# Shift and scale of adaLN with the weight tiles as the stationary operand, and a bank and a load size changed elsewhere, in a decoder-trunk kernel

## The chip, the cores and the metric

The kernel runs on one core of one Trainium2 chip. The metric is the device time of one execution in microseconds (us). It was measured three times for the kernel before.

## What is computed

One layer of a hybrid decoder trunk, for a prompt of 1024 tokens and 8 samples of 8 tokens (1088 columns in all). The part that the change touches most is the front of the layer:

```python
mod = jax.nn.silu(c) @ w_ada + b_ada
shift, scale, gate = jnp.split(mod, 3, axis=-1)
h = _rmsnorm(x, norm_g) * (1.0 + scale[:, None, :]) + shift[:, None, :]
parts = jnp.split(h @ w_in, _in_offsets(), axis=-1)
```

`c` has nine rows (one prompt, eight samples) of 1024; `w_ada` is 1024 x 3072. After that come three groups of dilated window attention, a state-space (SSD) branch whose output has a group RMSNorm over four groups, the two branch projections, the merge, and `x + gate * (merged @ w_out)` with a last RMSNorm.

## The kernel before

Everything is float32. The large products (`w_in`, `w_ssm`, `w_att`, `w_out`) are made of three products of a high and a low part in the type fp32r; `load_w` (lines 185 to 193) loads a weight tile and splits it on ACT and DVE. Small products run in plain float32, and the trace then shows two records (a weight load, PEld, and a matmul, PE) for one matmul of the code.

**Stage 0** (pool `ph0`, lines 291 to 368) makes `h`. Eight tiles `xT` (128 features x 1088 tokens) are squared on ACT, summed over features by PE (`sums`, line 165), and a root is taken (`rms`, `rsqrt`); PE spreads it over partitions into `rb` (line 356). `ada(q)` for q = 0 to 3 makes shift and scale of 256 features each. It loads two tiles `wa` of 1 MB and runs 32 matmuls (line 316): the stationary operand is `scT`, SiLU of the conditioning, 32 columns wide (nine of them filled), the moving operand is 128 columns of `w_ada`, and the four blocks j sit beside each other in four column groups of the array. So the result has sequences on partitions; ACT copies it (`row`, line 318), PE transposes it (line 320), and DVE adds and multiplies the biases into `mod` (lines 327 to 329). `modulate(f)` then makes `h_hi[f]` and `h_lo[f]` of one feature tile on DVE, ACT and POOL. `project_early` (line 242) begins two of the 96 projections of `w_in` while `h` is still being made: 144 matmuls that go through the feature tiles in pairs, 36 matmuls for two tiles.

Here and in the output stage the order of instructions is chosen by a scheduler ahead of time; each engine then works through its own list in order. All loads and stores are issued on one queue (SP), which holds eight transfers at a time.

**Attention and SSD** (a region in which PE's order is the order of the code, and in which the class `Order` mixes the small matmuls of the side branch into the stream of the projections by modelled costs). PSUM has eight banks; in the SSD part three belong to the projections (`bankPJ`), two to `bankA`, three to `bankB`, each handed round in turn. At the end of each of the four SSD groups PE sums squares (`sums`, line 165, called at line 967) into a bank named `ms`; DVE reads it at line 170. The next matmuls of the side branch are the transposes `tt` of the next group (three banks of `bankB`), later `cb` (two banks of `bankA`, one of `bankB`).

**Output stage** (lines 1114 on): five passes over eight column tiles. In pass 1, `ada_gate` (lines 466 to 480) makes the gate from eight tiles `wg` of 512 KB that share one buffer with the tile `smp`, which is filled in pass 4.

Of the kernel before, what the change touches and what calls it, by code (L numbers as in the profile page):

```python
# [9 lines left out]
F32 = mybir.dt.float32  # L10
F32R = mybir.dt.float32r
AF = mybir.ActivationFunctionType
# [4 lines left out]
D = 1024  # L17
T = 1024
# [92 lines left out]
def trunk(ctx: ExitStack, tc: tile.TileContext, I, O):  # L111
# [180 lines left out]
    with pool("ph0", 2) as p0:  # L292
# [13 lines left out]

        def ada(q):

            pr = bankB("ada")
            for k in range(0, 8, 4):  # L310
                wa = p0.tile([128, 4, 4, 128], F32, tag="wa", name="wa", bufs=6)
                SP.dma_start(out=wa.rearrange("p k j n -> p k (j n)"),
                             in_=I["w_ada"][q, k:k + 4].rearrange("k p n -> p k n"))
                for i in range(4):
                    for j in range(4):
                        PE.matmul(pr[j * 32:j * 32 + 32, :128], scT[:, k + i, :], wa[:, i, j, :], start=k + i == 0, stop=k + i == 7)
            row = p0.tile([128, 128], F32, tag="row", name="row")
            S.activation(row, pr[:, :128], AF.Copy)
            pt = bankB("adaT")
            PE.transpose(pt[:, :128], row, ident)  # L320
            fs = slice(2 * q, 2 * q + 2)
            pt = pt[:, :128].rearrange("p (i c n) -> p i c n", i=2, c=2)

            def each(ap):
                return ap[:, fs, None].to_broadcast([128, 2, 9])

            V.tensor_tensor(mod[:, 1, fs, :], pt[:, 1, :, :9], each(bs), op=OP.add)
            V.tensor_tensor(mod[:, 1, fs, :], mod[:, 1, fs, :], each(P("norm_g")), op=OP.mult)
            V.tensor_tensor(mod[:, 0, fs, :], pt[:, 0, :, :9], each(P("b_ada")), op=OP.add)
# [135 lines left out]

    def ada_gate(pool_, wgp, k, pg):

        wg = wgp.tile([128, D], F32, tag="smp", name="wg")
        SP.dma_start(out=wg, in_=I["w_gate"][k])
        for j in range(4):  # L470
            PE.matmul(pg[j * 32:j * 32 + 32, :256], scT[:, k, :], wg[:, j * 256:(j + 1) * 256], start=k == 0, stop=k == 7)
        if k < 7:
            return
        gt = pool_.tile([128, 256], F32, tag="gt", name="gt", bufs=1)
# [364 lines left out]
    with ExitStack() as bctx:  # L839
# [100 lines left out]
        def side():  # L940
            for gr in range(4):
# [21 lines left out]
                    order.passed.add(("x", xt))  # L963

                yield 7000.0,
                ps = bankB("ms")
                sums(ps, sq)
                ms = bp.tile([128, 3, QT], F32, tag="ms", name="ms", bufs=1)
                rms(ms, ps, 512)
# [151 lines left out]
    with pool("yr", 2) as yr, pool("yw", 2) as yw:  # L1121
# [27 lines left out]
        wlo = acp.tile([128, KO, D], F32R, name="wolo")  # L1149
        cut_psum("out", p=4, a=4)  # L1150
        pg = bankA("gate")
        mhi, mlo = [], []
        for gr in range(5):
            if gr:
                if gr < 4:
# [7 lines left out]
            for m in range(8):  # L1163
# [25 lines left out]
                if gr == 4:  # L1189

                    a, b = split(acc[m], 0.5)
                    mhi.append(a)
                    mlo.append(b)

                    if m == 0:
                        smp = acp.tile([128, KO, 2 * TS], F32R, tag="smp", name="smp")
                    S.activation(smp[:, m, :TS], a[:, T:].bitcast(F32), AF.Copy)
                    S.activation(smp[:, m, TS:], b[:, T:].bitcast(F32), AF.Copy)


    fp = ctx.enter_context(pool("fin", 1))
# [7 lines left out]
    for t in range(9):  # L1209
# [8 lines left out]
        for i in range(m):  # L1218
            ps = bankA("fo")
            cs = slice(i * w, (i + 1) * w)  # L1220
            if t == 8:

                for k in range(KO):
                    PE.matmul(ps[:, :w], smp[:, k, :], whi[:, k, cs], start=k == 0, stop=k == KO - 1)
                low = f2.tile([TS, w], F32, tag="low", name="low")
                S.activation(low, ps[TS:, :w], AF.Copy)
                V.tensor_tensor(low, low, gbs[:, cs], op=OP.mult)
                V.tensor_tensor(x[:n, cs], x[:n, cs], low, op=OP.add)
                for k in range(KO):
                    PE.matmul(ps[:n, :w], smp[:, k, :TS], wlo[:, k, cs], start=False, stop=k == KO - 1,  # L1230
                              skip_group_check=True)
            ps = ps[:n, :w]
            for k in range(KO if t < 8 else 0):
# [168 lines left out]
```

## Time and profile before

| what | value |
|---|---|
| median of 3 runs | 1892.5 us |
| lowest and highest | 1889.75, 1894.63 us |
| the profiled execution, its own time | 1892.67 us |
| its span, first to last instruction | 1890.6 us |
| time outside the span | 2.07 us |
| PE busy | 1853.4 us, 98% |
| DVE, ACT, POOL busy | 1020.6, 663.4, 271.5 us |
| mean granted TensorE clock | 0.994 of 2.4 GHz |

The profile is of one execution. A page gives busy times by engine and the costliest groups; the trace behind it is asked for stretches of time (windows), for waits, for a tile's instructions, and for the instructions in order of time (timeline). PE is TensorE's matmuls, PEld its weight loads, SPq the queue that issues transfers. A group of matmuls in a timeline row has its start, its length and its count (x32).

### The profile page before, as it was taken

How to read it: one execution, taken by the hardware profiler on the slowest of the kernel's cores; microseconds unless marked ns; L12 is line 12 of the kernel's file. 1: busy time of each engine (PE TensorE's matmuls, PEld its weight loads, DVE VectorE, ACT ScalarE, POOL GpSimd, SP SyncE). 2: the span in 40 equal slices, each digit the busy share in tenths (PEclk: the TensorE clock that was granted, in tenths of full speed). 3: DMA queues.
4: the chain of work that ended last, by engine and by line, in shares of the span. 5: the costliest groups of instructions: out<-in, count | busy, mean ns of one | idle time of the engine just before them, and what ended most of it. 6: DMA issues, size and time to landing. Idle time of an engine off the chain costs nothing.

```text
span 1890.6 us, 32497 instructions
## 1 busy us (share of the span) xinstructions
PE 1853.4 (98%) x13217; PEld 1736.5 (92%) x13217; DVE 1020.6 (54%) x1983; ACT 663.4 (35%) x1275; POOL 271.5 (14%) x445
## 2 busy tenths in 40 slices
PE   6999999999999999999999999999999999999998
PEld 4999999998999999999999999999999989999986
DVE  4633343325324322566776677577758656566655
ACT  4444223323423342423452435243534332131222
POOL 3100000000000000122322231233224200000400
PEclk8999999999999999999999999999999999999999
DMA  8422462273256227435453544443333364364322
GB/s 335 141 80 94 151 213 69 89 227 132 98 160 199 84 91 245 144 92 190 149 160 108 183 152 138 128 151 119 106 104 108 122 225 156 123 197 150 121 89 78
DMA packets 108870, 269.55 MB, mean 143 GB/s; under 512 B 41501, under 2 KB 50513, under 8 KB 105457
## 3 DMA queue, kind: packets, MB, share of 16 engines
q1 hardware_dynamic: 108720, 267.48, 43.1%
q8 instruction: 104, 1.70, 0.4%
q14 instruction: 46, 0.37, 0.1%
HBM read 224.93 MB, written 80.26 MB: 161 GB/s over the span
## 4 chain that ended last, share of the span: by engine, by line
PE 90%; DMA 5%; DVE 2%; issue 1%; ACT 1%; SPq 0%; POOL 0%; ACTq 0%; DVEq 0%
PE pj L198 23%; PE pj L199 22%; PE pj L200 22%; PE s L207 2%; PE o L207 2%; DMA csb<-cs_d 2%; PE pt L211 2%; PE yd L207 2%; PE yo L207 2%; PE fo L1237 2%; PE fo L1238 2%; PE fo L1236 2%; PE stt L207 1%; PE early L242 1%; PE tt L211 1%
## 5 line engine op out<-in xcount | busy, mean ns | idle before, releaser
L198 PE MATMUL pj<-h_hi,whi 128*128 128x368 f32 x2256 | 755.9, 335 | 0.4 <-ACT raw L870 0.4
L200 PE MATMUL pj<-h_lo,whi 128*128 128x368 f32 x2256 | 739.1, 328 | 0.0
L199 PE MATMUL pj<-h_hi,wlo 128*128 128x368 f32 x2256 | 738.9, 328 | 0.0
L198 PEld LDWEIGHTS pj<-h_hi,whi 128*128 128x128 f32 x2256 | 425.0, 188 | 17.1 <-issue 13.6
L199 PEld LDWEIGHTS pj<-h_hi,wlo 128*128 128x128 f32 x2256 | 424.9, 188 | 0.0
L200 PEld LDWEIGHTS pj<-h_lo,whi 128*128 128x128 f32 x2256 | 424.4, 188 | 0.0
L192 DVE TENSOR_TENSOR wlo<-wraw,whi 128x1024 fp32r<-128x1024 f32 (+1 forms) x136 | 149.8, 1101 | 191.0 <-ACT whi L191 189.0
L191 ACT ACTIVATE whi<-wraw 128x1024 fp32r<-128x1024 f32 (+1 forms) x136 | 126.5, 930 | 336.8 <-PE pj L200 283.6
L198 PE MATMUL pj<-yhi,whi 128*128 128x368 f32 (+1 forms) x480 | 157.3, 328 | 1.4 <-ACT yhi L1125 1.2
L199 PE MATMUL pj<-yhi,wlo 128*128 128x368 f32 (+1 forms) x480 | 157.6, 328 | 0.2 <-DVE wlo L192 0.2
L200 PE MATMUL pj<-ylo,whi 128*128 128x368 f32 (+1 forms) x480 | 155.6, 327 | 0.0
L649 DVE COPY pT<-pt 128x512 f32<-128x512 f32 x40 | 27.6, 690 | 147.4 <-PE pt L211 74.9
L630 ACT ACTIVATE pr<-pr,st 128x128 f32<-128x128 f32 (+1 forms) x192 | 83.6, 438 | 46.8 <-DVE st L627 46.8
L198 PEld LDWEIGHTS pj<-yhi,whi 128*128 128x128 f32 x480 | 90.1, 188 | 3.3 <-ACT yhi L1125 2.0
L199 PEld LDWEIGHTS pj<-yhi,wlo 128*128 128x128 f32 x480 | 90.1, 188 | 3.0 <-issue 2.1
L200 PEld LDWEIGHTS pj<-ylo,whi 128*128 128x128 f32 x480 | 89.9, 188 | 0.0
L887 DVE SCALAR_TENSOR_TENSOR xc<-raw,cw,xc 128x1112 f32<-128x1112 f32 x60 | 83.0, 1383 | 11.8 <-ACT xc L885 10.8
L980 DVE TENSOR_TENSOR csb<-tok,csb 128x2048 f32<-128x2048 f32 x16 | 37.1, 2317 | 75.1 <-DMA csb<-cs_d 75.1
L506 DVE COPY k<-pj 128x368 f32<-128x368 f32 (+2 forms) x44 | 23.9, 579 | 73.9 <-PE pj L200 70.7
L1011 POOL TENSOR_TENSOR xde<-xdt,tok 128x256 f32<-128x256 f32 x64 | 43.6, 709 | 133.8 <-DVE xdt L1004 133.8
L1067 POOL TENSOR_TENSOR sst<-sst,eall 128x256 f32<-128x256 f32 x64 | 49.9, 810 | 69.9 <-PE yo L207 67.6
L1034 DVE SCALAR_TENSOR_TENSOR sta<-sta,eall,stt 128x64 f32<-128x64 f32 x224 | 45.1, 271 | 26.8 <-ACT sta L1030 26.8
(275 smaller groups left out, 2396.4 us busy)
## 6 DMA issues: line engine op xcount, KB each, us to landing
wraw<-in_w_in SPq DMA_DIRECT2D x96, 512.0 KB
csb<-cs_d SPq DMA_DIRECT2D x16, 1088.0 KB
kt<-in_kc SPq DMA_DIRECT2D x32, 448.0 KB
out_kc<-in_kc SPq DMA_DIRECT2D x32, 448.0 KB
out_vc<-in_vc SPq DMA_DIRECT2D x28, 512.0 KB
vt<-in_vc SPq DMA_DIRECT2D x28, 512.0 KB
sg_d<-sg SPq DMA_DIRECT2D x16, 544.0 KB
ecs<-cs_d SPq DMA_DIRECT2D x32, 272.0 KB
```

The source lines that it names most:

```text
L191: S.activation(hi, raw, AF.Copy)
L192: V.tensor_sub(lo, raw, hi.bitcast(F32))
L198: PE.matmul(ps, whi[:, k, :], xhi[k], start=first and k == 0, stop=False)
L199: PE.matmul(ps, wlo[:, k, :], xhi[k], start=False, stop=False)
L200: PE.matmul(ps, whi[:, k, :], xlo[k], start=False, stop=last and k == n - 1)
L207: PE.matmul(out, w, x, **kw)
L211: PE.transpose(out, x, eye)
L630: S.activation(pr[:, h, c0:c0 + m], pr[:, h, c0:c0 + m], AF.Exp, scale=-1.0, bias=st[:, 0, h, u:u + 1], accum_out=st[:, 1, h, u:u + 1])
L887: V.scalar_tensor_tensor(c, raw[:, t:t + CONV], cw[:, j, t:t + 1], c, op0=OP.mult, op1=OP.add)
L1011: G.tensor_tensor(xde[:, c:c + 2].rearrange("p c (h d) -> p c h d", h=2), xdt[:, c:c + 2, :].rearrange("p c (h d) -> p c h d", h=2), tok[: ...
L1034: V.scalar_tensor_tensor(sta[:, i, hs], sta[:, i - 1, hs], eall[:, h0 + h, i:i + 1], ps[:, c, hs], op0=OP.mult, op1=OP.add)
L1067: G.tensor_tensor(part, part, etot[:, h0:h0 + 2, b:b + 2].rearrange("n h b -> n b h")[:, :, :, None] .to_broadcast([128, 2, 2, 64]), op=OP ...
```

## The change

In `ada` the weight tile `wa[:, i, j, :]` becomes the stationary operand, 128 columns, and the nine filled columns of `scT` move. The result has features on partitions, so the copy `row` and the transpose are gone, and one bank of `bankB` is used for each q in place of two. The sums at the end of an SSD group go to `bankA`. The gate's tiles are loaded in halves of 256 KB into two buffers, and `smp` is cut into two tiles accordingly.

```diff
         def ada(q):
-            pr = bankB("ada")
+            pt = bankB("ada")
             for k in range(0, 8, 4):
                 wa = p0.tile([128, 4, 4, 128], F32, tag="wa", name="wa", bufs=6)
...
                 for i in range(4):
                     for j in range(4):
-                        PE.matmul(pr[j * 32:j * 32 + 32, :128], scT[:, k + i, :], wa[:, i, j, :], start=k + i == 0, stop=k + i == 7)
-            row = p0.tile([128, 128], F32, tag="row", name="row")
-            S.activation(row, pr[:, :128], AF.Copy)
-            pt = bankB("adaT")
-            PE.transpose(pt[:, :128], row, ident)
+                        PE.matmul(pt[:, j * 32:j * 32 + 9], wa[:, i, j, :], scT[:, k + i, :9], start=k + i + j == 0,
+                                  stop=k + i == 7, skip_group_check=True)
...
-        wg = wgp.tile([128, D], F32, tag="smp", name="wg")
-        SP.dma_start(out=wg, in_=I["w_gate"][k])
-        for j in range(4):
-            PE.matmul(pg[j * 32:j * 32 + 32, :256], scT[:, k, :], wg[:, j * 256:(j + 1) * 256], start=k == 0, stop=k == 7)
+        for i in range(2):
+            wg = wgp.tile([128, D // 2], F32, tag="smp", name="wg", bufs=2)
+            SP.dma_start(out=wg, in_=I["w_gate"][k][:, i * 512:(i + 1) * 512])
+            for j in range(2 * i, 2 * i + 2):
+                PE.matmul(pg[j * 32:j * 32 + 32, :256], scT[:, k, :], wg[:, j % 2 * 256:(j % 2 + 1) * 256], start=k == 0,
+                          stop=k == 7)
...
                 yield 7000.0,
-                ps = bankB("ms")
+                ps = bankA("ms")
                 sums(ps, sq)
...
-                    if m == 0:
-                        smp = acp.tile([128, KO, 2 * TS], F32R, tag="smp", name="smp")
-                    S.activation(smp[:, m, :TS], a[:, T:].bitcast(F32), AF.Copy)
-                    S.activation(smp[:, m, TS:], b[:, T:].bitcast(F32), AF.Copy)
+                    if m % 4 == 0:
+                        smp.append(acp.tile([128, 4, 2 * TS], F32R, tag="smp", name="smp", bufs=2))
+                    S.activation(smp[-1][:, m % 4, :TS], a[:, T:].bitcast(F32), AF.Copy)
+                    S.activation(smp[-1][:, m % 4, TS:], b[:, T:].bitcast(F32), AF.Copy)
```

The change also moves instructions. PE's list in stage 0 before, from the sums of `x` on (`ms`): the first two `ada` blocks, then the first projections. The other two `ada` blocks follow after 19 and after 44 of the 144 matmuls of `early`.

```order
L165 MATMUL ms<-sqk,onesc 32x272 x32
L316 MATMUL ada<-wa,scT 32x128 x32
L356 MATMUL rb<-ms,onesc 128x272 x4
L320 MATMUL adaT<-pack,row 128x128
L316 MATMUL ada<-wa,scT 32x128 x32
L242 MATMUL early_459<-h_hi_90,whi 128x368
```

The same place in the changed kernel (its line 317 is the matmul of `ada`, 354 that of `rb`):

```order
L165 MATMUL ms<-sqk,onesc 32x272 x32
L317 MATMUL ada<-scT,wa 128x9 x20
L354 MATMUL rb<-ms,onesc 128x272
L317 MATMUL ada<-scT,wa 128x9 x2
L354 MATMUL rb<-ms,onesc 128x272
L317 MATMUL ada<-scT,wa 128x9 x2
L354 MATMUL rb<-ms,onesc 128x272
L317 MATMUL ada<-scT,wa 128x9 x2
L354 MATMUL rb<-ms,onesc 128x272
L317 MATMUL ada<-scT,wa 128x9 x102
L242 MATMUL early_443<-h_hi_90,whi 128x368
```

All 128 matmuls of `ada` now stand ahead of the first matmul of `early`.

PE's list between two SSD groups before, with the engines whose semaphores a row waits for in brackets (`ms` are the sums, `tt` the next group's transposes):

```order
L200 MATMUL pj<-h_lo_100,whi 128x368
L165 MATMUL ms<-sq,onesc 32x272 [waits Pool_49] x4
L211 MATMUL tt<-pack,xc 128x128 [waits DVE_49]
L211 MATMUL tt<-pack,xc 128x128 x7
L211 MATMUL tt<-pack,xcs 128x128 [waits DVE_49]
L198 MATMUL pj<-h_hi_93,whi 128x368
```

And now:

```order
L200 MATMUL pj<-h_lo_100,whi 128x368
L165 MATMUL ms<-sq,onesc 32x272 [waits DVE_49,Pool_49]
L165 MATMUL ms<-sq,onesc 32x272 [waits Pool_49] x3
L211 MATMUL tt<-pack,xc 128x128 [waits DVE_49]
L211 MATMUL tt<-pack,xc 128x128 x7
L211 MATMUL tt<-pack,xcs 128x128
```

The order is the same; the last transpose waits for nobody, and the first sum now waits for DVE too.

SP's list where the gate's loads begin, in the output stage, before (`yx` and `rb` feed the operands of the next pass, `wraw` is a weight tile):

```order
L469 DMA wg<-in_w_gate 128x1024
L1139 DMA yx<-u_d 128x1088
L1134 DMA rb<-rs_d 128x1088
L469 DMA wg<-in_w_gate 128x1024
L1139 DMA yx<-u_d 128x1088
L469 DMA wg<-in_w_gate 128x1024
```

And now:

```order
L468 DMA wg<-in_w_gate 128x512 x2
L1139 DMA yx<-u_d 128x1088
L468 DMA wg<-in_w_gate 128x512
L1134 DMA rb<-rs_d 128x1088
L468 DMA wg<-in_w_gate 128x512
L1139 DMA yx<-u_d 128x1088
L468 DMA wg<-in_w_gate 128x512
```

Two halves are asked for at the place of the first whole tile; the third and the fourth stand on both sides of `rb`.

## Rows read from the trace of the kernel before

**Rows 1.** The page, part 1: busy us, share, instructions.

```profile
PE 1853.4 (98%) x13217; PEld 1736.5 (92%) x13217; DVE 1020.6 (54%) x1983; ACT 663.4 (35%) x1275; POOL 271.5 (14%) x445
```

**Rows 2.** The chain of waits, 0 to 70 us: start, length, what.

```profile
13.20 16.52 DMA wa<-in_w_ada
56.35 6.23 PE early L242 x36
```

**Rows 3.** Timeline of PE, 17 to 37 us: start, length, operation, [idle before, releaser].

```profile
18.06 1.93 PE L316 MATMUL ada<-wa,scT 128*32 128x128 f32 x32 [1.17 <-DMA wa<-in_w_ada]
...
29.76 1.94 PE L316 MATMUL ada<-wa,scT 128*32 128x128 f32 x32 [0.70 <-DMA wa<-in_w_ada]
```

**Rows 4.** Timeline, 51 to 58 us: the last pair of feature tiles.

```profile
51.48 0.17 DVE L327 TENSOR_TENSOR mod<-adaT,bs 128x18 f32<-128x18 f32 x1
...
55.16 2.18 ACT L339 ACTIVATE h_hi<-xT,mod 128x1024 fp32r<-128x1024 f32 x2
```

**Rows 5.** Tile ada in 17.9:20.2, 20.6:22.6, 27:29.3, 36.8:38.8: ns min/median/max, starts.

```profile
L316 PEld LDWEIGHTS ada<-wa,scT x32: 127/177/178, 18.0 to 19.4; 128*32 128x32 f32 x32
...
L316 PEld LDWEIGHTS ada<-wa,scT x32: 110/168/177, 20.7 to 21.9; 128*32 128x32 f32 x32
...
L316 PEld LDWEIGHTS ada<-wa,scT x32: 125/177/177, 27.1 to 28.4; 128*32 128x32 f32 x32
...
L316 PEld LDWEIGHTS ada<-wa,scT x64: 106/110/110, 36.9 to 38.4; 128*32 128x32 f32 x64
```

**Rows 6.** Tile early in 31:36 and in 40:62.5: weight loads, ns.

```profile
L242 PEld LDWEIGHTS early<-h_hi,whi x8: 288/329/338, 31.6 to 34.9; 128*128 128x128 f32 x8
...
L242 PEld LDWEIGHTS early<-h_hi,whi x36: 186/188/189, 41.8 to 59.1; 128*128 128x128 f32 x36
```

**Rows 7.** Windows: length, busy us PE, PEld, DVE, ACT, POOL; clock, DMA, GB/s.

```profile
27.10:29.00 1.90, 1.87 (x32) 1.51 (x32) 1.77 (x5) 0.00 (x0) 1.53 (x3) 0.50 1.04 384
...
31.60:35.60 4.00, 4.00 (x17) 3.98 (x14) 1.35 (x2) 0.69 (x4) 3.71 (x10) 0.51 1.04 394
35.60:41.80 6.20, 6.19 (x90) 5.47 (x88) 3.05 (x5) 1.57 (x4) 3.63 (x6) 1.00 1.04 392
```

**Rows 8.** Timeline of the weight loads, 802.5 to 805 us.

```profile
802.62 1.92 PEld L207 LDWEIGHTS cb<-CT,xc 128*128 128x128 f32 x16
...
804.46 0.30 PEld L207 LDWEIGHTS cb<-CTs,xcs 128*128 128x128 f32 x2
...
804.68 0.19 PEld L198 LDWEIGHTS pj<-h_hi,whi 128*128 128x128 f32 x1
```

**Rows 9.** Windows, the end of the first transfers.

```profile
42.00:43.00 1.00, 1.00 (x7) 1.00 (x8) 1.00 (x1) 0.99 (x1) 0.00 (x0) 1.00 0.44 172
```

**Rows 10.** Waits of PE, 765 to 1530 us: total, times, longest.

```profile
PE tt L211 <- DVE ms L170: 5.9, 3, 2.6
```

**Rows 11.** Timeline, 968 to 990 us: the change from one SSD group to the next.

```profile
972.29 0.43 DVE L170 TENSOR_SCALAR ms<-ms 128x272 f32<-128x272 f32 x1
...
972.77 0.33 PE L211 MATMUL tt<-pack,xcs 128*128 128x128 f32 x1 [1.84 <-DVE ms L170]
...
987.35 1.95 PE L207 MATMUL cb<-CT,xc 128*128 128x128 f32 x16
```

**Rows 12.** Windows around two of those waits.

```profile
970.75:974.16 3.41, 1.57 (x11) 1.39 (x10) 1.97 (x4) 2.90 (x3) 0.54 (x2) 1.00 0.52 105
974.16:977.58 3.42, 3.42 (x13) 3.42 (x12) 2.75 (x2) 3.39 (x5) 0.00 (x0) 0.50 0.69 277
...
1158.48:1161.90 3.42, 3.42 (x13) 3.42 (x13) 1.89 (x2) 3.40 (x5) 0.00 (x0) 0.50 0.88 307
```

**Rows 13.** Waits of PE, 1500 to 1891 us; timeline at the first gate load.

```profile
PE gate L471 <- DMA wg<-in_w_gate: 3.1, 2, 1.7
...
1539.02 0.33 SPq L469 DMA_DIRECT2D wg<-in_w_gate  x1
...
1543.65 0.64 PE L471 MATMUL gate<-wg,scT 128*32 128x256 f32 x8 [1.65 <-DMA wg<-in_w_gate]
```

More of the change, by code (lines that the diff above doesn't have):

```diff
@@ L1151, in trunk @@
         pg = bankA("gate")
-        mhi, mlo = [], []
+        mhi, mlo, smp = [], [], []
         for gr in range(5):
@@ L1223, in trunk @@
                 for k in range(KO):
-                    PE.matmul(ps[:, :w], smp[:, k, :], whi[:, k, cs], start=k == 0, stop=k == KO - 1)
+                    PE.matmul(ps[:, :w], smp[k // 4][:, k % 4, :], whi[:, k, cs], start=k == 0, stop=k == KO - 1)
                 low = f2.tile([TS, w], F32, tag="low", name="low")
@@ L1229, in trunk @@
                 for k in range(KO):
-                    PE.matmul(ps[:n, :w], smp[:, k, :TS], wlo[:, k, cs], start=False, stop=k == KO - 1,
+                    PE.matmul(ps[:n, :w], smp[k // 4][:, k % 4, :TS], wlo[:, k, cs], start=False, stop=k == KO - 1,
                               skip_group_check=True)
```

## The prediction

> **What bounds the kernel now.** I read the page first. PE is busy for 98% of the span, and its weight loads run beside the matmuls for 92% [rows 1]. So nearly everything that shortens or lengthens PE's own list shows in the time, and idle time of the other engines is worth something only where PE waits for them. Three places remain to be read: the start, the changes between SSD groups, and the gate.
>
> In the start the chain of waits goes through the transfers of `wa` and then through the matmuls of `early`, whose last 36 take 6.23 us and end at 56.35 + 6.23 = 62.58 us [rows 2]. The timeline shows where PE is before that: `ada` at 18.06, when its first tile has landed, a second tile's worth with the rest of q = 0, then q = 1 up to 29.76 + 1.94 [rows 3], and then `early`, from 31.6 us on. From there PE is practically never idle, and `ada` of q = 2 and 3 lies between matmuls of `early`. All transfers of the start have landed by about 42.5 us (a busy share of 0.44 in the window from 42 to 43) [rows 9].
>
> The clock matters here. It was low (0.50) while `ada` ran at 27.1, and through the first 4.0 us of `early`; then it was high [rows 7]. The records of `ada` tell the same: a load of 32 columns takes 177 ns at the low clock and 110 ns at the high one. At 18.06 it takes 177 ns as well, so the clock was low there too; in the second block it falls to 110 ns, so the clock rose for a while near 22 us, and was low again at 27.1 [rows 5].
>
> **The start, step by step.** Removed are four copies, four transposes, and 256 records of `ada` with 32 columns to load and 128 to move. Added are 256 records (128 matmuls, two records each) with 128 columns to load and nine to move. What such a record costs is set by its load. The nearest rows are those of `cb`, plain float32 with 128 stationary columns: 16 loads, each followed by 128 moving columns, go from 802.62 to 804.46, which is 115 ns each; two, followed by 64 columns, go from 804.46 to 804.68, 110 ns each [rows 8]. Halving the moving columns saves 5 ns, so nine columns gain no more: 110 ns at the high clock.
>
> At the low clock no row has such a stream, and I bound it from two sizes. A load of 128 columns takes 329 ns low and 188 ns high [rows 6], one of 32 columns 177 and 110 [rows 5]. The 96 columns between them cost 152 ns low and 78 ns high, so 128 columns cost 203 ns low and 104 high; scaled by the measured 110 over 104 the low value is 215 ns. I take 207 ns, between 203 and 215.
>
> Which clock will it be? In the rows of before it rose twice in the start: once during the second block of `ada`, whose records move 128 columns each and follow closely on the first block [rows 5], and once after 4.0 us of `early`, whose records move 352 or 368 [rows 7]. In between a block of the same `ada` at 27.1 did not lift it [rows 7], and at 972 it fell after PE had stood still for 1.84 us [rows 11, 12]. The new stretch moves nine columns every 0.2 us and begins at the low clock. That is less moving work than in any stretch of the trace in which the clock rose. I take the low clock for all of it.
>
> So `ada` takes 256 x 207 ns = 53.0 us from 18.06 on. Four small matmuls of `rb` lie between them; with 0.7 us for these, which is a choice, it ends at 71.8 us. The transfers are not in the way: all are landed by 42.5 us, and the two late tiles of `wa` have to wait only for the first two tiles' matmuls.
>
> The order decides the rest. All 128 matmuls of `ada` stand ahead of the first of `early`, so `early`, which had done its first half beside waits for the other engines, now begins at 71.8 us. It then needs 4 x 6.23 = 24.9 us at the high clock [rows 2], and 2.0 us more because its first 4.0 us run at half speed, as they did before [rows 7]. The last pair of `h` is not late: before, its `h_hi` were done 5.9 us after its `mod` (51.48 to 55.16 + 2.18) [rows 4], and now `early` comes to that pair 18.7 us after it begins. So `early` ends at 71.8 + 24.9 + 2.0 = 98.7 us instead of 62.58: **+36.1 us**. The copies and transposes that go were hidden: ACT's copies lay beside matmuls of `early`, and four transposes are worth 0.1 us each. What follows is PE's list in the same order, so the delay stays to the end.
>
> The Trainium skill gives one formula for a weight load ("TensorE: Matmul & The Clock Gate", section "LDWEIGHTS (loading the stationary operand)"): columns over 1.2 GHz, 107 ns for 128, with no clock in it. The rows agree with that at the high clock and not at the low one, where the load takes 329 ns in place of 188; by the formula `ada` would end some 25 us earlier, which is the second rival below.
>
> **The SSD groups.** The last transpose `tt` takes the bank that `ms` still held until DVE read it at 972.29 [rows 11]. It waited three times, 5.9 us in all [rows 10]. After two of these waits the clock went down, from 974.16 to 977.58 and from 1158.48 to 1161.90, 3.42 us each at 0.50 [rows 12]; that is 3.4 us of work lost. With `ms` in `bankA` the transpose waits for an older bank. The new wait, of the first sum for DVE, is for a read of the tile `yd` that was done with the group's last output, before the sums' own input `sq`, and the next user of the bank of `ms` is the second half of `cb`, 15 us after DVE's read [rows 11]. So nothing takes the place of the wait: **-9.3 us**. The bounds are 0, if PE then meets a later wait for the same DVE, and -9.3.
>
> **The gate.** PE waited twice for the gate's tiles, 3.1 us in all; the first was asked for at 1539.02 and used at 1543.65 [rows 13]. Now two halves are asked for at that place, which brings no byte of the second half earlier, and the third half waits for the first one's matmuls as the second tile did. There are twice as many switches between these matmuls and the stream of `pj`. I take 0, between -3.1 and +3.1. The split of `smp` changes neither the number of copies nor that of matmuls: 0.
>
> **The sum.** The profiled execution took 1892.67 us, 2.07 us of it outside the span; the median of the three runs is 1892.5 us, so the two are one number. 1892.67 + 36.1 - 9.3 + 0 = **1919.5 us**.
>
> **Rivals.**
> 1. *The clock is released during the weight loads* (not slower). If PE's steady work lifts the clock 3.9 us after 18.06, as the two blocks did before, 19 records run at 207 ns and 237 at 110 ns: `ada` ends at 18.06 + 3.9 + 26.1 + 0.7 = 48.8 us. `early` begins at the high clock and ends at 73.7, +11.1, and with -9.3 the time is 1894.5 us. For it speaks that PE and PEld never stop in that stretch, while the clock rose near 22 us in spite of a gap. Against it: so few columns move. The point from which it decides: a total of no more than 15 us in place of 36.1, that is a mean record below some 120 ns. 15%.
> 2. *The loads keep their pace at the low clock.* Then `ada` ends at 18.06 + 28.2 + 0.7 = 47.0 us, `early` ends at 73.9, and the time is 1894.7 us. The rows on loads at both clocks speak against it. 9%. This is what the page's formula says.
> 3. *The loads hide altogether and only the data bound the start.* `early` begins at 42.8 us, when the last tile has landed, and ends at 67.7 at best: +5.1 - 9.3 - 3.1 gives 1885.4 us, faster. The rows of `cb` speak against it. The Trainium skill excludes float32 from fast weight loads (same page, "Weight-path perf modes"); no run here shows such a load. 4%.
> 4. *A load does not begin while a nine-column matmul is under way.* Then a record costs its whole 329 ns, 84.2 us in all, and the time is 1950.7 us. Against it: in rows 8 loads of 190 ns follow each other every 110. 4%.
> 5. *The SSD wait moves instead of going.* The sum without -9.3 is 1928.8 us at the low clock. It is taken into the forecast's own range.
>
> **How the numbers follow.** The forecast, low clock throughout, has 66%; its own range is 1910 to 1929 us (1914 by the bounds of load and gate, 1910 if the clock rises for a part of the stretch, 1929 if the SSD wait moves). What is left, 2%, is other mishaps. To hold 8 in 10 the range has to take in rivals 1 and 2 down to 1892: 1892 to 1929 us. A difference of 0.3%, 5.7 us, is about what a measurement of this kernel can tell from no change. Faster by more than that needs rival 3 or one of the first two with luck at the gate: 6%. Rivals 1 and 2 lie within it, less the cases in which a part of the 9.3 us is kept: 16%. Slower: the forecast, rival 4, the mishaps and the rest of the first two: 78%.
>
> **What would show it.** In the trace of the changed kernel: `ada` as one stretch of 256 records from 18 us on, its loads about 330 ns long and 207 ns apart, the granted clock 0.50 to its end, the first `early` at about 72 us and the last ending at about 99; no wait of `tt` for DVE at line 170, and no fall of the clock at the two group changes; waits for the gate's tiles of 0 to 6 us in all. The prediction is wrong if the clock rises inside the stretch of `ada` (then `early` begins before 60 us), or if the records come 110 ns apart at the low clock.

## The result and the profile after

The changed kernel takes **1932.4 us** (median of 4 runs, 1930.24 to 1933.01); the kernel before, run beside it, 1891.1 us (median of 4, 1887.71 to 1894.63). The ratio is 1.0218, 95% interval 1.0206 to 1.0230: slower by 39 to 43.5 us. The forecast was 1919.5 us, with a range from 1892 to 1929. The direction and the place were right; the size was not, and the time lies 3.4 us outside the range.

The profiled execution took 1930.24 us, its span 1928.3 us, 37.7 more than the span of before (1890.6). The page, part 1 (busy us, share, instructions), as in [rows 1]:

```profile
PE 1903.8 (99%) x13213; PEld 1784.3 (93%) x13213; DVE 1021.9 (53%) x1983; ACT 662.7 (34%) x1271; POOL 278.1 (14%) x445
```

PE has 50 us more of busy time for the same result, and 13 us less of idle time: what the change cost is PE's own. The chain of waits (start, length, what) shows the start, where [rows 2] had the transfers of `wa` and then `early`:

```profile
18.01 8.68 PE ada L317 x40
34.34 43.62 PE ada L317 x204
77.96 25.77 PE early L242 x144
```

`ada` stands in one stretch ahead of all of `early`, as forecast; 204 of its records take 43.62 us, 213.8 ns each. `early` ends at 103.73 us instead of 62.58: **+41.1 us**. Between the two lines of `ada` lie the four `rb` matmuls, one at a time. The timelines of PE and of the weight loads (start, length, operation, [idle before, releaser]):

```profile
26.61 1.27 PE L354 MATMUL rb<-ms,onesc 1*128 1x272 f32 x2
27.81 1.02 PE L317 MATMUL ada<-scT,wa 128*128 128x9 f32 x4
```

```profile
28.77 0.50 PEld L354 LDWEIGHTS rb<-ms,onesc 1*128 1x128 f32 x2
29.96 0.93 PEld L317 LDWEIGHTS ada<-scT,wa 128*128 128x128 f32 x4 [0.70 <-issue]
```

From 26.61 to the next `ada` at 27.81 are 1.2 us, and behind each `rb` the next load of `ada` begins 0.70 us late. Four times over, with the few records of `ada` between them, the stretch loses 5 us.

The instructions of the tile `ada` (ns min/median/max, first and last start):

```profile
L317 PEld LDWEIGHTS ada<-scT,wa x256: 287/333/337, 18.0 to 77.5; 128*128 128x128 f32 x128
```

333 ns is the length of a load at the low clock [rows 6: 329 low, 188 high], and it holds from the first records to the last.

The SSD groups: the sums of the first group come 41.1 us later than before (969.2 to 1010.3), those of the last 36.0 us later (1519.7 to 1555.7), so **5.1 us** were won there. The list of PE's waits over the whole span (total, times, longest), to compare with [rows 10, 13]:

```profile
PE ms L165 <- ACT sqk L346: 7.7, 7, 6.4
PE pj L198 <- ACT yhi L1125: 2.1, 1, 2.1
PE yo L207 <- DVE sta L1034: 2.1, 2, 1.2
PE vt L211 <- DVE oT L825: 1.6, 3, 0.5
```

The wait of `tt` for line 170 is gone, with both falls of the clock behind it, and so are the waits for `wg`. But `yo` (a matmul of the SSD branch) now waits 2.1 us for the states `sta` that DVE makes (0.4 before), and in the output stage `pj` waits 2.1 us for `yhi`, an operand of the next pass (1.2 before), and behind each the clock falls. Windows (length, busy us of PE, PEld, DVE, ACT, POOL; granted clock, DMA, GB/s):

```profile
1460.90:1464.30 3.40, 3.31 (x13) 3.31 (x14) 3.40 (x11) 0.90 (x1) 1.17 (x1) 0.50 0.07 19
1576.90:1580.70 3.80, 3.80 (x14) 2.58 (x14) 2.62 (x3) 1.11 (x1) 0.00 (x0) 0.55 0.72 234
```

From the last sums to the end, **1.8 us** were lost (the last matmul of `fo`, the last product, at 1919.1 instead of 1881.3, +37.8). The three parts, 41.1 - 5.1 + 1.8, make up the 37.7 us between the spans. The medians lie 41.2 us apart, since the profiled execution is the shortest of its four; the traces do not show where the other 3.5 us are.

### The profile page after: what moved, and what is told of

Same layout as the page of the kernel before. It is cut to its first block, busy times and chain, and to the rows that moved or that the text cites. A ratio compares the mean times of both kernels' runs of the same rounds, so it can differ in the third digit from the quotient of the medians.

```text
span 1928.3 us, 32494 instructions
## 1 busy us (share of the span) xinstructions
PE 1903.8 (99%) x13213; PEld 1784.3 (93%) x13213; DVE 1021.9 (53%) x1983; ACT 662.7 (34%) x1271; POOL 278.1 (14%) x445
## 4 chain that ended last, share of the span: by engine, by line
PE 95%; DMA 2%; DVE 2%; issue 1%; ACT 1%; SPq 0%; ACTq 0%; DVEq 0%
PE pj L198 23%; PE pj L199 22%; PE pj L200 22%; PE ada L317 3%; PE s L207 2%; PE o L207 2%; PE pt L211 2%; PE yd L207 2%; PE yo L207 2%; PE fo L1237 2%; PE fo L1238 2%; PE fo L1236 2%; PE stt L207 1%; PE early L242 1%; PE tt L211 1%; DMA csb<-cs_d 1%
## 5 line engine op out<-in xcount | busy, mean ns | idle before, releaser
L980 DVE TENSOR_TENSOR csb<-tok,csb 128x2048 f32<-128x2048 f32 x16 | 37.9, 2368 | 75.5 <-DMA csb<-cs_d 75.5
L1188 POOL TENSOR_TENSOR acc<-acc,ta 128x368 f32<-128x368 f32 (+1 forms) x24 | 24.2, 1009 | 247.7 <-DVE ta L1187 247.7
```

## The experiments

Each kernel was run beside the kernel before on the same chip. "Early ends" is the start of the matmul behind the last of `early`; the next columns are the first and last `ms` sum of the SSD groups and the last matmul of `fo`, all in us of the profiled execution.

```
version                               median   ratio to before, 95%     early  ms first  ms last  fo last
before                                1891     -                         62.5    969.2   1519.7   1881.3
the change                            1932.4   1.0218 (1.0206, 1.0230)  103.7   1010.3   1555.7   1919.1
1  without the new ada                1887.2   0.9985 (0.9976, 0.9994)   62.7    970.2   1513.0   1878.5
2  new ada alone                      1935.0   1.0238 (1.0220, 1.0257)  104.7   1012.5   1564.1   1925.4
3  bank of ms alone                   1882.4   0.9964 (0.9952, 0.9977)   61.7    968.6   1512.3   1873.4
3b the same again                     1885.1   0.9970 (0.9959, 0.9981)   61.4    968.8   1513.4   1873.9
4  gate halves, two smp alone         1893.6   1.0021 (1.0011, 1.0031)   61.6    968.1   1515.6   1881.7
5  change, 128 columns moving         1903.1   1.0061 (1.0041, 1.0081)   75.5    982.4   1525.7   1890.3
6  change, 32 columns moving          1932.1   1.0213 (1.0196, 1.0230)  102.8   1009.8   1556.3   1921.2
7  change, early between ada          1928.9   1.0191 (1.0172, 1.0210)  102.5   1010.2   1556.9   1922.3
8  change, rb together                1930.5   1.0200 (1.0183, 1.0218)   99.0   1006.9   1551.0   1919.2
9  1, gate matmuls together           1883.5   0.9961 (0.9949, 0.9972)   61.5    967.2   1510.5   1873.0
10 3, gate loads later                1884.7   0.9966 (0.9953, 0.9979)   62.1    968.6   1512.7   1874.1
11 new ada repaired, bank of ms       1898.8   1.0036 (1.0024, 1.0049)   74.0    980.6   1526.4   1887.8
```

### 1 to 4: the change taken apart

Experiment 1 is the change with `ada` as it was:

```diff
-            pt = bankB("ada")
+            pr = bankB("ada")
...
-                        PE.matmul(pt[:, j * 32:j * 32 + 9], wa[:, i, j, :], scT[:, k + i, :9], start=k + i + j == 0,
-                                  stop=k + i == 7, skip_group_check=True)
+                        PE.matmul(pr[j * 32:j * 32 + 32, :128], scT[:, k + i, :], wa[:, i, j, :], start=k + i == 0, stop=k + i == 7)
+            row = p0.tile([128, 128], F32, tag="row", name="row")
+            S.activation(row, pr[:, :128], AF.Copy)
+            pt = bankB("adaT")
+            PE.transpose(pt[:, :128], row, ident)
```

> The change without its new shift and scale: norm sums in the other bank, gate weights in halves, two smp tiles. Theory (the loss is the start's, and the parts add up): the traces put +41.1 us on the start, -5.1 on the SSD part, +1.8 to 2.2 on the gate, so without the first this kernel is 3 us faster than before (1888). Rival A (the new start also set where the later waits and clock falls came, and without it the SSD part gains the forecast 9.3): about -9 to -7 (1883). Rival B (the later parts carry some of the loss whatever the start does): slower than before.

Experiment 2 is the kernel before with the opposite of that edit and nothing else.

> Before with the new shift and scale alone. Theory: the early projections end about 41 us later, at 103.7 instead of 62.6 us, and the program is longer by that, 1932 us; the loads follow 213 ns apart. Rival (part of the 41 us is made up later, in waits for data that a later start no longer has): +30 to +37. Rival B (the pauses at the four rb pairs come from another part of the change): +36.

Experiment 3 is the kernel before with one line changed:

```diff
-                ps = bankB("ms")
+                ps = bankA("ms")
                 sums(ps, sq)
```

> Before with the norm sums' bank alone. Theory (the wait for VectorE is gone, but a new one for the states appears and is followed by a clock fall): -5 us. Rival A (the new wait came only with the later start): -9.3, the whole of the 5.9 us of waits and 3.4 us of clock falls. Rival B (the waits come back as waits for another buffer): 0.

Experiment 4 is the kernel before with the change's `ada_gate` and `smp`:

```diff
-        wg = wgp.tile([128, D], F32, tag="smp", name="wg")
-        SP.dma_start(out=wg, in_=I["w_gate"][k])
-        for j in range(4):
+        for i in range(2):
+            wg = wgp.tile([128, D // 2], F32, tag="smp", name="wg", bufs=2)
+            SP.dma_start(out=wg, in_=I["w_gate"][k][:, i * 512:(i + 1) * 512])
+            for j in range(2 * i, 2 * i + 2):
...
-                    if m == 0:
-                        smp = acp.tile([128, KO, 2 * TS], F32R, tag="smp", name="smp")
+                    if m % 4 == 0:
+                        smp.append(acp.tile([128, 4, 2 * TS], F32R, tag="smp", name="smp", bufs=2))
```

> Before with the gate weights in halves and two smp tiles alone. Theory (the waits for the gate weights go, 4.8 us of them, and their place is taken by a clock fall ahead of the gate's first matmuls): +2 us. Rival A (that fall belongs to the later start or the other bank): -3, what the waits for the halves save. Rival B (hidden either way): 0.

Measured by the medians: new `ada` alone +44.8 us, bank of `ms` alone -7.9 (and -5.4 when run again), gate parts alone +3.4; together 40 to 43, and the whole change is +41.2. The new `ada` alone costs more than the 41 expected: its `early` ends 42.2 us late, and behind it the clock falls three times (near 1200, 1470 and 1586 us) where it fell twice before (974 and 1158). Without the new `ada` the rest is 3 us faster than before. So the parts add up within their intervals, the loss is the new `ada`'s, and rival B of the first expectation is out: the rest does not lose. The bank alone is not worth 0; whether it is worth the 5 us of its expectation or the 9.3 of rival A, its two intervals do not decide. For the gate the size came near the expected 2 us, and the reason did not come: PE waits 4.0 us for `wg` in experiment 4, 3.1 before.

In the SSD part (first to last `ms` sum) the kernel before takes 550.5 us, experiment 4, whose bank of `ms` is the old one, 547.5, and experiment 3 takes 543.7. Experiment 4 has 5.4 of the 5.9 us of the old waits, but its clock never fell behind one of them (no load of `pj` lasts over 247 ns there, where a fall makes it 334); so of the 6.8 us between before and experiment 3 some 2.5 to 3 are the two falls, and the rest the waits. PE's waits in experiment 3 between 930 and 1535 us, where [rows 10] had 5.9 us of `tt`:

```profile
PE pj L198 <- ACT yhi L1125: 1.2, 1, 1.2
PE pj L198 <- ACT raw L870: 1.2, 1, 1.2
PE yo L207 <- DVE sta L1034: 1.1, 1, 1.1
```

Of the 5.9 us that went, 0.7 came back at `sta` and 1.2 at `raw` (an input tile of the SSD branch). In five kernels with the new `ada` (the change, 2, 6, 7, 11) the wait for `sta` is 1.5 to 2.1 us long and the clock falls behind it; those of them with the new bank take 545.4 to 546.7 us in this part, 5 and 8, which have the new `ada` and no fall there, 543.3 and 544.1. The length of the wait does not decide it: it is 1.7 us in 8 and 1.6 in 3b, without a fall. Why the fall comes in five of the seven kernels with the new `ada` and in none without it was not found: 11, whose start is only 11.5 us late, has it, and 8, 36.5 us late, has not.

### 5 and 6: more columns moving

```diff
-                        PE.matmul(pt[:, j * 32:j * 32 + 9], wa[:, i, j, :], scT[:, k + i, :9], start=k + i + j == 0,
+                        PE.matmul(pt[:, j * 128:j * 128 + 128].rearrange("p (r n) -> p r n", r=4), wa[:, i, j, :],
+                                  scT[:, k + i, None, :].to_broadcast([128, 4, 32]), start=k + i + j == 0,
...
-            pt = pt[:, :128].rearrange("p (i c n) -> p i c n", i=2, c=2)
+            pt = pt[:, :512].rearrange("p (i c n) -> p i c n", i=2, c=2)
```

> The change, but 128 columns move at each of ada's matmuls (the vectors with their zeros, four times over) in place of nine. Theory (the clock stays at the low level because nine columns leave TensorE's array idle between loads): the clock rises, the loads take 188 ns in place of 333, the records follow some 110 ns apart in place of 213, and the early projections end about (213 - 110) x 256 = 26 us sooner, near 77, although 14 times as many columns move; time about 1906. Rival (it is the loads that take 213 ns at any clock, or the low clock has another cause): the pace is 213 ns or more, by as much as the 107 ns that 128 columns take at the low clock, time 1932 to 1960.

Experiment 6 has `scT[:, k + i, :]`, 32 columns, in place of the nine and is otherwise the change.

> The change with 32 columns moving in place of nine (the vectors with their zeros). Theory: 32 columns beside 128 of a load still leave the array mostly idle, the clock stays low and the pace at 213 ns, for the columns lie beside the next load: 1932, as the change. Rival (any activity above nine columns lifts the clock): pace near 110 ns, early projections end near 77, 1906. Rival B (columns and loads follow one another): pace 213 + 19 = 232 ns, 5 us more.

With 128 columns the records are 113 ns apart (172 in 19.40 us) and `early` ends 28 us sooner, at 75.5, near the 77 expected; the time falls by 29 us. The tile `ada` and the chain of waits in experiment 5:

```profile
L317 PEld LDWEIGHTS ada<-scT,wa x256: 186/192/333, 17.9 to 54.1; 128*128 128x128 f32 x128
```

```profile
17.89 6.29 PE ada L317 x40
28.71 19.40 PE ada L317 x172
48.11 2.82 PE early L242 x17
50.93 3.57 PE ada L317 x32
54.50 21.02 PE early L242 x127
```

The first loads still take 333 ns, then they take 192, the length at the high clock: with fourteen times the moving columns nearly every load is shorter. (The scheduler here put the last 32 records behind the first `early`.) With 32 columns the clock does not rise. A window in experiment 6 (columns as above):

```profile
34.50:77.50 43.00, 43.00 (x203) 43.00 (x204) 16.61 (x22) 7.76 (x12) 13.13 (x26) 0.50 0.21 79
```

PE is busy for 43.00 of 43.00 us and has the clock at 0.50, the lower of its two levels (1.2 of 2.4 GHz); the pace is that of nine columns. So the loads are slow because the clock is low, and the clock followed the moving columns: with 9 and with 32 of them behind each load it stayed low, with 128 it rose, and in none of the three does PE stand still in this stretch. (Of the 128 columns 36 are filled, of the 32 nine; whether the number of columns counts or what is in them was not tested.) The Trainium skill ("TensorE: Matmul & The Clock Gate", section "HAM oscillation — how this bites in real kernels") traces a clock that falls again and again to gaps in which PE waits for data; here the clock stays low without a gap, and the measurement decides.

### 7: early projections between the blocks of ada

```diff
-        for k, a, b in passes():
+        for n, (k, a, b) in enumerate(passes()):
+            if n % 6 == 0:
+                yield
...
+            if q == 1:
+                side = project_early(js, ws, ([bankPJ] * 3, [bankA, bankA, bankC]))
+                next(side)
             for f in (2 * q, 2 * q + 1):
                 modulate(f)
-        project_early(js, ws, ([bankPJ] * 3, [bankA, bankA, bankC]))
+            if q:
+                next(side)
+        for _ in side:
+            pass
```

> The change with the early projections written between ada's blocks: blocks 0 and 1, early 0, block 2, early 1, block 3, early 2 and 3. The same matmuls. Theory (the price is in the low clock; early projections bring it to the high level, and a block of 64 records behind them runs at the high level for a part at least): early projections end between 92 (both later blocks at 110 ns) and 106 (both at 213 ns and the clock brought up anew each time), against 103.7 in the change. Rival (the loss is the order, early projections that stood in gaps of ada before and now stand behind it, not the pace of the loads): the order of before is restored in part, so the end comes near 75 or sooner.

`early` ends at 102.5 us, 1.2 us sooner than in the change: near the upper end of what the theory gave (92 to 106), and nowhere near the 75 of the rival. Windows in experiment 7: the head of the third block of `ada` (59.23 to 69.22 us), the rest of it, and most of the last block:

```profile
59.30:62.40 3.10, 3.10 (x30) 3.10 (x29) 0.00 (x0) 0.00 (x0) 0.00 (x0) 1.00 0.00 0
62.50:69.20 6.70, 6.70 (x35) 6.70 (x34) 0.00 (x0) 0.00 (x0) 0.00 (x0) 0.53 0.00 0
...
81.00:87.80 6.80, 6.80 (x34) 6.80 (x33) 0.00 (x0) 0.00 (x0) 0.00 (x0) 0.50 0.00 0
```

The loads in the head of the third block and in the last one (ns min/median/max, first and last start):

```profile
L319 PEld LDWEIGHTS ada<-scT,wa x30: 188/192/192, 58.9 to 62.2; 128*128 128x128 f32 x30
...
L319 PEld LDWEIGHTS ada<-scT,wa x32: 333/333/333, 80.8 to 87.4; 128*128 128x128 f32 x32
```

The third block shows both paces: behind `early` its loads begin 114 ns apart at a clock of 1.00, then the clock falls inside the block. Where it is low, as in the last block, they begin 213 ns apart. (The counts of a window take in the records that its edges cut.) What the high clock saves at the head of a block, the next `early` pays for the most part, until the clock is up again: 36 of its matmuls take 7.91 us there, and 6.23 at the high clock [rows 2]; all 144 take 31.2 us, and 25.77 in the change. The order alone is not the loss.

### 8: the rb matmuls together

The loop that makes `rb` was moved, unchanged, out of the part with high priority to just behind `ada(0)`; its four matmuls then stand together.

```diff
-            for j in range(4):
-                ps = (bankPJ if j < 3 else bankC)("rb")
...
             ada(q)
             if q == 0:
+                for j in range(4):
+                    ps = (bankPJ if j < 3 else bankC)("rb")
...
```

> The change with the four rb matmuls together behind ada's first block; in the change they stand one by one between ada's matmuls, at 1.2 us of the path each. Theory (about half of that is the pause at each change between a load of one row and one of 128): together they cost some 1.4 us at the low clock and one pause of 0.7, 2.1 in place of 4.8, early projections end near 101.0. Rival (the matmuls themselves are slow at the low clock, the pauses are overlap): 4 x 1.2 again, 103.7.

The chain of waits in experiment 8:

```profile
18.11 13.11 PE ada L317 x64
32.44 41.06 PE ada L317 x192
73.50 25.55 PE early L242 x144
```

Between 31.22 and 32.44 the four take 1.2 us, as much as one of them cost alone; `early` ends at 99.0, 4.7 us sooner than in the change, more than the 2.7 expected: 4.0 us of it are the four matmuls, and most of the rest are the first records of `ada`, which ran before the clock fell at 18.9 us. The rival is out. The median fell by 1.9 us only (1930.5); what the start won is lost again behind the last sums, where this execution waits 3.9 us for `wg` and the change not at all (`fo` ends at 1919.2 and 1919.1).

### 9 and 10: the gate

Experiment 9 is experiment 1 with both halves asked for first and the four matmuls behind them:

```diff
-        for i in range(2):
-            wg = wgp.tile([128, D // 2], F32, tag="smp", name="wg", bufs=2)
-            SP.dma_start(out=wg, in_=I["w_gate"][k][:, i * 512:(i + 1) * 512])
-            for j in range(2 * i, 2 * i + 2):
+        wg = [wgp.tile([128, D // 2], F32, tag="smp", name="wg", bufs=2) for i in range(2)]
+        for i in range(2):
+            SP.dma_start(out=wg[i], in_=I["w_gate"][k][:, i * 512:(i + 1) * 512])
+        for j in (2, 3, 0, 1):
...
```

> The norm sums' bank and the gate parts (no new shift and scale), but the four gate matmuls of a step stand together behind both halves' loads: 10 groups of gate matmuls in PE's order, against 13 with the halves apart and 9 before. Theory (a group costs some 0.56 us of TensorE whether it has 2, 4 or 8 records, so more groups is what the halves cost): 3 x 0.56 = 1.7 us better than the halves apart (which gave -3.0 against before), so about -5. Rival (the cost is in the loads, two transfers in place of one, or in the two smp tiles): -3 as before.

It is 7 us faster than before, experiment 1 was 3: the intervals (0.9949 to 0.9972, 0.9976 to 0.9994) do not touch. Beside experiment 3b, which has the bank alone and ran with it (0.9970 and 0.9961), neither the halved transfers nor the two `smp` tiles cost anything that can be told; the halves' matmuls, apart, do. The timeline of PE in experiment 4, where they are apart:

```profile
1538.57 0.63 PE L472 MATMUL gate<-wg,scT 128*32 128x256 f32 x4 [1.41 <-DMA wg<-in_w_gate]
1539.13 0.94 PE L200 MATMUL pj<-ylo,whi 128*128 128x368 f32 x4
1539.99 0.63 PE L472 MATMUL gate<-wg,scT 128*32 128x256 f32 x4
1540.55 0.43 PE L198 MATMUL pj<-yhi,whi 128*128 128x368 f32 x1
```

In the kernel before, where they are together, eight begin at 1543.65 [rows 13], and the next matmul is this:

```profile
1544.22 0.43 PE L198 MATMUL pj<-yhi,whi 128*128 128x368 f32 x1
```

Four records take 0.56 us of PE's list (1538.57 to 1539.13), eight take 0.57. A group of two costs 0.55. At the high clock a group costs the same whatever its size, and with the halves there are 13 of them in PE's order instead of 9: 2.2 us. Experiment 4 is 3.4 us slower than before (2.1 to 5.9 by its interval); in its profiled execution, which is 4.5 us behind between the last sums and the end, 0.9 us more of waiting for `wg` and a fall of the clock from 1546 to 1549 (1.7 us) add to these 2.2. Between experiments 1 and 9 the groups (13 and 10) make 1.7 us and the waits for `wg` (3.3 and 1.9) make 1.4, of 3.9 by the medians; the rest was not found.

Experiment 10 is experiment 3 with each load of `wg` issued behind the load of the same step's `vhi`:

```diff
-    def ada_gate(pool_, wgp, k, pg):
+    def ada_gate(pool_, wgp, k, pg, d):
...
-        SP.dma_start(out=wg, in_=I["w_gate"][k])
+        with tc.issue_after(d.ins):
+            SP.dma_start(out=wg, in_=I["w_gate"][k])
...
-                vhi, vlo, _ = load_w(I["w_ssm"][gr, m] if gr < 4 else I["w_att"][m], 4, 128, yw)
+                vhi, vlo, d = load_w(I["w_ssm"][gr, m] if gr < 4 else I["w_att"][m], 4, 128, yw)
...
```

> The norm sums' bank alone, and the load of each gate weight issued behind the load of its step's own output weights, so that the gate matmuls stand one group per step (8 groups) and none where the second stage's rows are first waited for. Theory (the gate weights are waited for at that border, 1.3 + 2.7 us, and their 0.5 MB each take bandwidth from the rows awaited there): 3 to 5 us faster than the norm sums' bank alone (which gave -7.9 against before), so -11 to -13. Rival (the rows of the next group are awaited there anyway; PE waits for them in place of the gate weights): -8, with longer waits for yhi.

The gate's matmuls now begin at 1580 us and wait for nothing, and the time is that of experiment 3 (0.9966 beside 0.9970 in the same runs): the rival. PE's waits from 1500 us on in experiment 10:

```profile
PE pj L198 <- ACT yhi L1126: 3.3, 2, 1.8
PE pj L198 <- DVE acc L1184: 1.0, 1, 1.0
```

At that border PE waits for the rows of the next pass whether gate matmuls stand there or not. In this kernel the waits for `wg` that the profile listed were worth nothing.

> The norm sums' bank alone, once more beside the other two. Theory: -7.9 us again (-9 to -5). Rival (the first value was luck of where the clock fell): -5 or less.

Run a second time, experiment 3 gave -5.4 us against the before of its runs, at the edge between the two; its interval (0.9959 to 0.9981) and the first one's overlap. I put the bank of `ms` at 4 to 9 us.

### 11: the new form, repaired

This kernel has 128 columns moving (as in 5) and `rb` behind the first block (as in 8), with the new bank of `ms`, and `ada_gate` and `smp` as before; each edit is the one shown there:

```diff
+                        PE.matmul(pt[:, j * 128:j * 128 + 128].rearrange("p (r n) -> p r n", r=4), wa[:, i, j, :],
+                                  scT[:, k + i, None, :].to_broadcast([128, 4, 32]), start=k + i + j == 0,
...
-                ps = bankB("ms")
+                ps = bankA("ms")
```

> The new shift and scale with 128 columns moving and the rb matmuls together behind its first block, with the norm sums' bank and without the gate parts. Theory (at the high clock a record of the new form still takes 113 ns of TensorE against 60 of the old, and TensorE is now busy from 18 us on, so what is saved in waits cannot pay for it): early projections end near 73, some 11 us behind before; with 7 us from the norm sums' bank, 4 us slower than before (1894.5). Rival (with the clock up, the ordering fills the old waits for data and the new form is level): early projections end near 63 to 66, 1884 to 1887.

The start came as expected, the end 4 us later than expected: 1898.8 us, 0.36% slower than before. The chain of waits:

```profile
18.68 9.25 PE ada L317 x64
27.93 0.67 PE rb L359 x8
28.61 18.06 PE ada L317 x160
46.67 2.81 PE early L242 x17
49.48 3.57 PE ada L317 x32
53.05 21.02 PE early L242 x127
```

PE goes from 18.68 to 74.07 without a stop. At the high clock a record of the new form takes 113 ns (160 in 18.06 us), and one of the old form some 24 ns, for 64 loads of 32 columns begin between 36.9 and 38.4 us [rows 5]. (The expectation's 60 ns is the old form at the low clock, 32 in 1.94 us [rows 3].) In PE's list the new form takes 30.9 us here (9.25 + 18.06 + 3.57) and the old form took 11.1 in the kernel before, in spite of the low clock in three of its blocks of 32 records. That is 20 us more, and the kernel before stood still for 6.0 us of waits for `wa` and ran the first 4.0 us of `early` at the low clock [rows 7]; so only some 8 of the 20 are hidden: `early` ends 11.5 us late. Of the 4.3 us beyond the expectation a fall of the clock behind `sta` (1432 to 1436 us) took some 2; the SSD part lasts 545.8 us, 2.1 more than in experiment 3. So the new form loses here even with the clock up. Faster than both kernels are those without it: 3, 9 and 10, 1882 to 1885 us, which do not differ by more than their intervals, and by 3 us experiment 1.

## Why the prediction was wrong in its size

**Low clock through all of `ada`: right.** The deciding step, "I take the low clock for all of it", held, and experiments 5 and 6 show why: more moving columns, and nothing else, brought the high clock. Rival 1 (the clock released) did not come with nine columns or with 32: the loads of 333 ns tell it. Rival 2 (loads keep their pace at the low clock, which the formula in the Trainium skill, "TensorE: Matmul & The Clock Gate", section "LDWEIGHTS (loading the stationary operand)", gives) is refuted: 213.8 ns against 113. Rival 3 and rival 4 did not come either: 1932 us is far from 1885, and 213.8 ns is no 329.

**The load's pace: 207 ns taken, 213.8 measured**, inside the bounds of 203 and 215. Over 256 records +1.7 us.

**"With 0.7 us for these, which is a choice": the step that failed most.** The four `rb` matmuls took 5.2 us of PE's list (59.95 us from the first `ada` to the first `early`, less 256 x 213.8 ns). 0.7 us was their length in the kernel before, where they stood together and the granted clock was 1.00:

```profile
22.24 0.74 PE L356 MATMUL rb<-ms,onesc 1*128 1x272 f32 x8
```

In the change they stood alone between loads of another shape, at the low clock, and each paid a pause. PE's order was known; that each change of shape has a price, and that the low clock raises it, was not looked for. +4.5 us.

**`early`: 26.9 us forecast, 25.77 measured**, -1.1 us. The three make +36.1 into +41.1.

**"So nothing takes the place of the wait": half wrong.** The wait and both falls went, but PE then met `sta` (1.7 us more than before) and a new fall (1.7 us of work lost): -5.1 us instead of -9.3, between the bounds of 0 and -9.3 that the prediction gave, and its rival 5 in part. These two leave 0.8 us that no row explains. Alone, the bank gives 6.8 us in this part (5.9 in 3b).

**"I take 0" for the gate: +1.8 us**, inside its bounds. That there are "twice as many switches" was seen but given no price; it is 0.56 us for each added group, 2.2 for four. In the profiled execution the fall behind the wait for `yhi` (1.7) and the longer wait itself (0.9) come to these, and the 3.1 us of waits for `wg` go off: +1.7 in all.

The errors are +5.0, +4.2 and +1.8 us, each in the same direction; with them the forecast becomes 1930.5 us, and the profiled execution, the shortest of its four, took 1930.24. The median is 2 us above that, so that the sum meets it so closely is in part luck of the execution. (The lower end by load and gate is 1919.5 - 1.0 - 3.1 = 1915.4 us, not 1914; nothing hangs on it.) The range's upper end, 1929, was made from one of them alone, the wait that moves; with the bounds of load, SSD and gate added it would have reached 1929 + 2 (215 ns) + 3.1, which holds the result, though none of these bounds is one for the `rb` matmuls.

## What to carry to other kernels

Before a small operand is made the moving one, look at the granted clock of that stretch and at the length of its loads: here a stream of loads with 9 or 32 columns behind each ran at the low clock though PE never idled, and padding the moving side to 128 columns gave 29 us back. Count the changes between matmuls of different shape in PE's order, not the matmuls: here four in a row cost what one alone did. And before work is moved away from a wait, look at which wait ends next behind it; the gate's loads were waited for at a place where PE would have waited anyway.

## What the runs showed that was not expected

The granted clock in the windows can be wrong. In the change the stretch of `ada` reads 1.00:

```profile
34.50:77.50 43.00, 43.00 (x203) 43.00 (x203) 16.89 (x22) 7.77 (x12) 13.13 (x26) 1.00 0.22 80
```

The same window in experiment 6 reads 0.50, with the same 203 records in it and the same 333 ns for a load. The change's trace does not tell of the low level there; the length of a known instruction tells the clock, the column alone does not. (So does experiment 5: its clock reads 1.00 from 18 to 21 us, and its loads last 333 ns there.)

A change of shape in PE's order has a price of its own, and for `rb` it goes with the clock. At the low clock a lone `rb` costs 1.20 us in the change, 0.70 of it the pause before the next load of `ada`. At the high clock, in experiment 5, it costs 0.65 us (24.18 to 24.83), 0.36 of it the pause:

```profile
24.11 0.29 PEld L355 LDWEIGHTS rb<-ms,onesc 1*128 1x128 f32 x2
24.76 0.52 PEld L317 LDWEIGHTS ada<-scT,wa 128*128 128x128 f32 x4 [0.36 <-issue]
```

Four together cost 1.22 us at the low clock (experiment 8) and 0.67 at the high one (experiment 11), as much as one alone. So the 0.7 us of the prediction had both wrong: the low clock makes 1.2 of it, and four places make that 4.8; the rest of the 5.2 lies in the few records of `ada` between them (four in 0.95 us). A group of `gate` matmuls costs 0.56 us at the high clock, whether it has four records or eight; in the change the first such group, at the low clock, takes 1.00 (1579.26 to 1580.26).
